# Splitting the memory rows of a cross-attention in four steps beside the units of the attention before it

## The chip, the core and the metric

The kernel runs on one core of a Trainium2 chip. Time is device time in microseconds (us) for one execution of the whole layer. The core has a matmul engine (TensorE, PE in the profile, with its weight loads shown apart as PEld), a vector engine (VectorE, DVE), an activation engine (ScalarE, ACT), GpSimd (POOL) and a queue that issues transfers (SyncE, SP). Each engine takes its instructions in the order in which the program lists them for that engine; between engines they wait on semaphores.

## The reference, cut to what matters

One decoder layer on 512 tokens of width 1024, all in float32:

```
x = x + 0.5 * swiglu(rmsnorm(x), gate, up, down)               # FFN 1, hidden width 2816
h = rmsnorm(x); z = h @ w_in                                   # 2560 columns
y_a = spatial gating of z[:, :1024], groups of 64, chunks of 128
y_b = causal attention, 8 heads of 64, three dilations summed by their softmax denominators
x = x + concat(rmsnorm(y_a), rmsnorm(y_b)) @ w_out
h = rmsnorm(x); m = rmsnorm(mem) * mem_norm                    # mem: 256 rows of width 1024
x = x + softmax((h @ wq) @ (m @ wk).T / 16) @ (m @ wv) @ wo    # cross-attention, 4 heads
x = x + 0.5 * swiglu(rmsnorm(x), gate, up, down)               # FFN 2
out = rmsnorm(x)
```

The change concerns m: the 256 normalised rows of the memory, which the cross-attention needs for its keys and values and which depend on nothing that the layer computes before.

## The kernel before

Activations are held transposed: feature blocks of 128 on the partitions, tokens along the free axis. Every product is made three times: each operand is split into a high part (rounded to the matmul's format) and a low part (the rest), and `mm3` (L124 to L129) adds high by high, high by low and low by high in PSUM. A split costs one ACTIVATE on ACT for the high part (L103) and one subtraction on DVE for the low part (L104). Weights come in by `load_weight` (L109): a transfer on SP into `wraw`, then a split into `whi` and `wlo`; each of the three has 3 buffers, so a weight's buffers hold up the loads behind it until its low part has been made and its matmuls are done.

The stages follow each other as in the reference: FFN 1, `mixers`, `cross`, FFN 2. In `mixers` the heads are worked off in 32 units (4 head pairs m, 2 heads r of a pair, 4 blocks i of 128 query rows). A unit u goes through three functions, and the loop at L617 to L626 runs them with a lag:

- `scores(u)`: three matmuls of 256 to 512 columns into a PSUM bank `aux` (4 banks), then on DVE the mask and the row minimum (L523), on ACT the exponential (L527), on DVE the reciprocal (L530) and the scaling (L531).
- `transposes(u - 3)`: up to four PE transposes (L539) into another `aux` bank, and a split into `pt` on ACT and DVE.
- `values(u - 4)`, for every second unit: 6 or 12 matmuls of 256 columns into an `aux` bank, and a split into `yH` and `yL` (L570, L571) with a square (L574). After the last block of a head pair, at the units 7, 15, 23 and 31, the squares are added up; two of these additions run on POOL (L170).

L523 is thus what gives a score's PSUM bank back, and its block of 128 columns (i = 0) marks the start of four units in the trace: the first, fifth, ninth and so on.

Two pieces of work lie between the units. At `u == 12` `qk_transpose(1)` makes queries and keys of the second half of the heads (L453). At `u == 16` `mem_split` (L389) loads the memory rows in four transfers (L393, tile `mraw`, which takes the four buffers of tag `qk` when `qk_transpose` has read them for the last time), and for each of the four transfers multiplies two row blocks by the norm's gain and factor on DVE (L395, 2 instructions), and splits the pair into `mH` (ACT, L103) and `mL` (DVE, L104). It returns the lists that `cross` (L673) uses for its values and keys.

The order of the instructions on each engine is not written out by hand: a scheduler lays it out when the program is built, by what is ready in its own estimate of time, and the earlier line of the program goes first among what is ready. So the first half of the output projection (`mix_out`, part 0, L631 to L640: 8 weight loads, 96 matmuls of 512 columns in all, an addition to `x` on DVE for each of 8 blocks), which needs only the gating's output, is found in the trace between the attention's matmuls; so are its splits of weights (`wlo`) on DVE.

Of the kernel before, what the change touches and what calls it, by code (L numbers as in the profile page):

```python
# [17 lines left out]
F32 = mybir.dt.float32  # L18
# [6 lines left out]
P = 128  # L25
S = 512
D = 1024
KD = D // P
# [4 lines left out]
NM = 256  # L33
# [5 lines left out]
LAG = 3  # L39
WARM = 20  # L40
SB = 6
LINE = 512

FILL = 56
# [10 lines left out]
def body(tc, I, out):  # L55
    nc = tc.nc
    from contextlib import ExitStack
    ctx = ExitStack()
    with ctx:
# [27 lines left out]
        def gcol(off, k):  # L87
            return gains[:, off + k:off + k + 1]
# [13 lines left out]
        def split(hi, lo, src):  # L102
            ins = nc.scalar.activation(hi, src, AF.Copy)  # L103
            nc.vector.tensor_sub(lo, src, f32(hi))  # L104
            return ins
# [281 lines left out]
            return h[0][k][:, ts], h[1][k][:, ts]  # L387

        def mem_split(pool, big, mR):  # L389
            mH, mL = (big.tile([P, KD, NM], F32R, name=n, tag="t8", bufs=4) for n in ("mH", "mL"))  # L390
            for k in range(0, KD, 2):
                raw = pool.tile([P, 2, NM], F32, name="mraw", tag="qk", bufs=4)
                nc.sync.dma_start(raw, I["memT"][k:k + 2].rearrange("k p n -> p k n"))  # L393
                for j in range(2):
                    nc.vector.scalar_tensor_tensor(raw[:, j], raw[:, j], gcol(G_MEM, k + j), mR,  # L395
                                                   op0=ALU.mult, op1=ALU.mult)
                split(mH[:, k:k + 2], mL[:, k:k + 2], raw)
            return [mH[:, k] for k in range(KD)], [mL[:, k] for k in range(KD)]

        def mixers(norm, cs, big):  # L400
            col = []
            hshape = [P, 8, 64]
            with tc.tile_pool(name="mix", bufs=1) as mp:
                lng = mp.tile([P, S], F32, name="lng", tag="s2", bufs=SB)
                lnb = mp.tile([P, S], F32, name="lnb", tag="s2", bufs=SB)
                nc.sync.dma_start(lng, I["ln"][0:1, :].to_broadcast([P, S]))
# [23 lines left out]
                qk = {}  # L430
# [18 lines left out]
                def qk_transpose(b):  # L449
                    for m in range(4):  # L450
                        ps = aux_tile()
                        for t in range(NT):
                            nc.tensor.transpose(ps[:, t * P:(t + 1) * P],  # L453
                                                qk[t][:, m * P:(m + 1) * P], ident_b)
                        if m >= 2:
                            hi, lo = h_tile("qkH"), h_tile("qkL")
                            split(hi, lo, ps)
                            kT[2 * b + m % 2] = (hi, lo)
                            continue


                        qT[2 * b + m % 2] = []
                        for r in range(2):
                            hi, lo = h_tile("qkH"), h_tile("qkL")
                            rows, other = (slice(x * 64, (x + 1) * 64) for x in (r, 1 - r))
                            for x in (hi, lo):
                                nc.gpsimd.memset(f32(x[other]), 0.0)
                            split(hi[rows], lo[rows], ps[rows])
                            qT[2 * b + m % 2].append((hi, lo))
# [19 lines left out]
                for t in range(NT):  # L489
# [3 lines left out]
                    nc.vector.tensor_sub(vt, vt, mu[:, t, :, None].to_broadcast(hshape))  # L493
                    sq = mp.tile([P, S], F32, name="vsq", tag="s2", bufs=SB)
                    nc.scalar.activation(sq, V[:, t], AF.Square)
# [18 lines left out]
                def scores(u):  # L514
                    m, r, i = units[u]
                    n = (i + 1) * P
                    N = max(n, 256)
                    sc = aux_tile()
                    mm3(sc[:, :N], qT[m][r], kT[m], (slice(None), slice(i * P, (i + 1) * P)),
                        (slice(None), slice(0, N)), True, True)  # L520
                    s = mp.tile([P, S], F32, name="s", tag="s2", bufs=SB)
                    nmx = sm.tile([P, 1], F32, name="nmx", tag="nmx")
                    nc.vector.tensor_tensor_reduce(  # L523
                        out=s[:, :n], in0=sc[:, :n], in1=const[:, C_MASK + S - n:C_MASK + S],
                        scale=-ATT_SCALE, scalar=3e38, op0=ALU.add, op1=ALU.min, accum_out=nmx)
                    Z = sm.tile([P, 1], F32, name="Z", tag="Z")
                    nc.scalar.activation(s[:, :n], s[:, :n], AF.Exp, bias=nmx, scale=-1.0,  # L527
                                         accum_out=Z)
                    rz = sm.tile([P, 1], F32, name="rz", tag="rz")
                    nc.vector.reciprocal(rz, Z)  # L530
                    nc.vector.tensor_scalar_mul(s[:, :n], s[:, :n], rz)  # L531
                    prob[u] = s

                def transposes(u):
                    m, r, i = units[u]
                    s = prob.pop(u)
                    tr = aux_tile()
                    for kt in range(i + 1):
                        nc.tensor.transpose(tr[:, kt * P:(kt + 1) * P],  # L539
                                            s[:, kt * P:(kt + 1) * P], ident)  # L540
                    if i % 2 == 0:
                        pts[m, r, i // 2] = tuple(
                            mp.tile([P, 4, 256], F32R, name="pt", tag="t4", bufs=4)
                            for _ in range(2))
                        for p in pts[m, r, i // 2]:
                            nc.gpsimd.memset(f32(p[:, i + 1, 0:P]), 0.0)
                    pt = pts[m, r, i // 2]
                    c0 = (i % 2) * P
                    split(pt[0][:, :i + 1, c0:c0 + P], pt[1][:, :i + 1, c0:c0 + P],
                               tr.rearrange("p (k c) -> p k c", k=4)[:, :i + 1])  # L550

                def values(u):
                    m, r, i = units[u]
                    if i % 2 == 0:
                        return
                    rows = slice(r * 64, (r + 1) * 64)
                    pv = aux_tile()
                    pt = pts.pop((m, r, i // 2))
                    for kt in range(i + 1):
                        mm3(pv[:, :256], (vH[kt], vL[kt]), pt,  # L560
                            (slice(None), slice(m * P, (m + 1) * P)),
                            (slice(None), kt), kt == 0, kt == i)
                    if r == 0 and i == 1:
                        yH[4 + m], yL[4 + m] = h_tile("yH"), h_tile("yL")
                        sqs[m] = base.tile([P, S], F32, name="sqb", tag="sq" if m else "sqacc",
                                           bufs=3 if m else 1)
                    o = pv[rows, :256]
                    c = slice((i - 1) * P, (i + 1) * P)
                    g = gcol(G_OB, m)[rows]
                    nc.scalar.activation(yH[4 + m][rows, c], o, AF.Copy, scale=g)  # L570
                    nc.vector.scalar_tensor_tensor(yL[4 + m][rows, c], o, g,  # L571
                                                   f32(yH[4 + m][rows, c]),
                                                   op0=ALU.mult, op1=ALU.subtract)
                    nc.scalar.activation(sqs[m][rows, c], o, AF.Square)  # L574
                    if r == 1 and i == NT - 1:
                        stats.take(sqs[m])

                def gate_mix():
# [11 lines left out]
                    for t in range(NT):  # L590
                        sq = mp.tile([P, S], F32, name="usq", tag="s2", bufs=SB)
                        nc.scalar.activation(sq, U[:, t], AF.Square, accum_out=ssa[:, t:t + 1])
# [24 lines left out]
                for u in range(LAG, nu + LAG + 1):  # L617
                    if u == nu // 2 - LAG - 1:
                        qk_transpose(1)
                    if u == nu // 2:  # L620
                        mem["split"] = mem_split(mp, big, mem["R"])
                    if u < nu:
                        scores(u)
                    transposes(u - LAG) if u - LAG < nu else None
                    if u > LAG:
                        values(u - LAG - 1)  # L626
# [20 lines left out]
        mem = {}  # L647
# [157 lines left out]
        with tc.tile_pool(name="big", bufs=1) as big:  # L805
            y = mixers(n2, cs[0], big)
            cross(n3, y, mem["split"], n4, big)
# [86 lines left out]
```

## Time and profile before

| | |
|---|---|
| median of 3 runs | 1131.15 us (1131.06 to 1132.29) |
| the profiled execution: its own time | 1132.03 us |
| its span, first to last instruction | 1130.3 us |
| mean granted clock of PE | 0.994 |
| PE busy | 1113.1 us, 98% of the span |
| DVE busy | 592.8 us, 52% |
| ACT busy | 424.6 us, 38% |
| POOL busy | 74.8 us, 7% |
| transfers | 110.79 MB, 98 GB/s on average |

Times in the trace count from the first instruction. The profiled execution is one execution with a time of its own, which lies 0.88 us above the median of the runs; 1.73 us of it lie outside the span. Busy shares are averages over all stages. The attention of `mixers` lies between about 490 and 563 us. In a list of instructions, a row holds the start, the duration, the engine, the line, the operation, what is written and read, and the shape; a bracket behind it gives the idle time of the engine before it and what ended it. In a table of stretches, a row holds the stretch, its length, the busy time of PE, PEld, DVE, ACT and POOL with the instructions in brackets, the granted clock, the share of the transfer engines and GB/s.

### The profile page before, as it was taken

What the parts mean: (1) busy time and instruction counts of PE and PEld (TensorE: products, weight loads), DVE (VectorE), ACT (ScalarE), POOL (GpSimd) and SP (SyncE); (2) the same over time, 40 slices, a digit from 0 to 9 for tenths busy, and PEclk for the clock granted to TensorE, in tenths of its full rate; (3) what the DMA queues carried; (4) which work ended last, traced back from release to release, by engine and by line L of the source; (5) the groups of instructions that cost most, each with busy time, mean ns of one, the idle gap of its engine ahead of it and who ended that gap; (6) DMA issues with size and microseconds to landing.
All of it is one profiled execution on the core that took longest, in us unless ns stands there. A gap on an engine that the chain in (4) does not pass through costs nothing. (4 is left out here: it accounts for less than half of the span.)

```text
span 1130.3 us, 13961 instructions
## 1 busy us (share of the span) xinstructions
PE 1113.1 (98%) x5472; PEld 934.5 (83%) x5472; DVE 592.8 (52%) x1027; ACT 424.6 (38%) x672; POOL 74.8 (7%) x98
## 2 busy tenths in 40 slices
PE   9999999999999999999999999999999999999996
PEld 7788888888888888887878988778888888888996
DVE  4544533444444447579897555455444334455542
ACT  6332312232234333567655344333232222333420
POOL 2000100000002200011121000120000000000011
PEclk9999999999999999999999999999999999999998
DMA  6322333222233422111136421232332333223511
GB/s 220 112 94 89 114 91 131 99 93 93 77 92 111 149 93 95 38 48 38 57 103 205 150 71 60 60 109 80 107 93 66 102 113 109 96 93 114 155 64 38
DMA packets 39698, 110.79 MB, mean 98 GB/s; under 512 B 4432, under 2 KB 9296, under 8 KB 39632
## 3 DMA queue, kind: packets, MB, share of 16 engines
q1 hardware_dynamic: 39632, 109.89, 30.5%
q8 instruction: 43, 0.70, 0.2%
q14 instruction: 23, 0.19, 0.1%
HBM read 107.78 MB, written 2.10 MB: 97 GB/s over the span
## 5 line engine op out<-in xcount | busy, mean ns | idle before, releaser
L103 ACT ACTIVATE whi<-wraw 128x1024 fp32r<-128x1024 f32 (+2 forms) x213 | 202.8, 953 | 519.6 <-PE acc L128 292.5
L104 DVE TENSOR_TENSOR wlo<-wraw,whi 128x1024 fp32r<-128x1024 f32 (+2 forms) x213 | 236.9, 1114 | 162.7 <-ACT whi L103 162.5
L127 PE MATMUL acc<-hH,whi 128*128 128x512 f32 x768 | 300.6, 391 | 0.0
L128 PE MATMUL acc<-hL,whi 128*128 128x512 f32 x768 | 299.2, 390 | 0.8 <-DVE hL L203 0.7
L129 PE MATMUL acc<-hH,wlo 128*128 128x512 f32 x768 | 299.1, 389 | 0.5 <-DVE wlo L104 0.5
L128 PEld LDWEIGHTS acc<-hL,whi 128*128 128x128 f32 x768 | 144.2, 188 | 32.2 <-DVE hL L203 2.2
L127 PEld LDWEIGHTS acc<-hH,whi 128*128 128x128 f32 x768 | 144.2, 188 | 30.9 <-issue 0.5
L129 PEld LDWEIGHTS acc<-hH,wlo 128*128 128x128 f32 x768 | 144.2, 188 | 30.6 <-DVE wlo L104 1.0
L127 PE MATMUL acc<-hidH,whi 128*128 128x512 f32 (+1 forms) x308 | 115.5, 375 | 0.0
L129 PE MATMUL acc<-hidH,wlo 128*128 128x512 f32 (+1 forms) x308 | 115.2, 374 | 0.0
L128 PE MATMUL acc<-hidL,whi 128*128 128x512 f32 (+1 forms) x308 | 115.2, 374 | 0.0
L170 POOL TENSOR_TENSOR sq<-sq 128x512 f32<-128x512 f32 (+1 forms) x39 | 49.4, 1266 | 774.2 <-ACT sq L178 773.7
L247 DVE TENSOR_TENSOR u<-acc,R 128x512 f32<-128x512 f32 x44 | 30.4, 690 | 121.6 <-PE acc L129 121.6
L243 DVE TENSOR_TENSOR gp<-acc,R 128x512 f32<-128x512 f32 x44 | 30.4, 691 | 85.5 <-PE acc L129 81.7
L127 PEld LDWEIGHTS acc<-hidH,whi 128*128 128x128 f32 x308 | 58.0, 188 | 10.3
L129 PEld LDWEIGHTS acc<-hidH,wlo 128*128 128x128 f32 x308 | 58.0, 188 | 10.3
L128 PEld LDWEIGHTS acc<-hidL,whi 128*128 128x128 f32 x308 | 58.0, 188 | 10.3
L127 PE MATMUL acc<-whi,hH 128*128 128x512 f32 x160 | 62.5, 390 | 0.0
L129 PE MATMUL acc<-whi,hL 128*128 128x512 f32 x160 | 62.3, 389 | 0.0
L128 PE MATMUL acc<-wlo,hH 128*128 128x512 f32 x160 | 62.3, 389 | 0.0
L230 DVE SCALAR_TENSOR_TENSOR x<-acc,x 128x512 f32<-128x512 f32 (+1 forms) x40 | 23.3, 584 | 73.9 <-PE acc L129 73.9
L178 ACT ACTIVATE sq<-x 128x512 f32<-128x512 f32 (+1 forms) x48 | 26.1, 551 | 40.7 <-DVE x L230 38.0
(213 smaller groups left out, 1490.0 us busy)
## 6 DMA issues: line engine op xcount, KB each, us to landing
wraw<-up SPq DMA_DIRECT2D x44, 512.0 KB, 3.5
wraw<-gate SPq DMA_DIRECT2D x43, 512.0 KB, 3.4
wraw<-down SPq DMA_DIRECT2D x28, 384.0 KB, 3.1
wraw<-w_in SPq DMA_DIRECT2D x20, 512.0 KB, 3.5
wraw<-down SPq DMA_DIRECT2D x28, 320.0 KB, 2.8
wraw<-w_out SPq DMA_DIRECT2D x16, 256.0 KB, 2.6
wraw<-wv SPq DMA_DIRECT2D x8, 512.0 KB, 3.5
wraw<-wk SPq DMA_DIRECT2D x8, 512.0 KB, 4.5
```

The lines of the kernel that those rows point to most:

```text
L103: ins = nc.scalar.activation(hi, src, AF.Copy)
L104: nc.vector.tensor_sub(lo, src, f32(hi))
L127: nc.tensor.matmul(ps, lhsT=aH, rhs=bH, start=start, stop=False)
L128: nc.tensor.matmul(ps, lhsT=aH, rhs=bL, start=False, stop=False)
L129: nc.tensor.matmul(ps, lhsT=aL, rhs=bH, start=False, stop=stop)
L170: nc.gpsimd.tensor_add(self.parts[0], self.parts[0], sq)
L178: nc.scalar.activation(sq, src, AF.Square)
L230: nc.vector.scalar_tensor_tensor(X[d][:, tok], acc, 0.5, X[d][:, tok], op0=ALU.mult, op1=ALU.add)
L243: nc.vector.tensor_mul(gp, ps[0], R)
L247: nc.vector.tensor_mul(u, ps[1], R)
```

## The change

`mem_split` becomes a generator. Its first call allocates `mH` and `mL`, issues all four transfers one behind the other and enters the lists of `mH` and `mL` in `mem`; each of the four calls that follow does one of the four pairs of row blocks: two L395 multiplications, the ACT copy and the DVE subtraction. The first call stands at unit 16, where the whole function stood; the others stand at the units 20, 23, 26 and 29, in the loop ahead of that unit's `scores`. No instruction is added or taken away.

```diff
--- before.py
+++ after.py
@@ -39,6 +39,8 @@
 LAG = 3
 WARM = 20
 SB = 6
+
+MEM_AT = (16, 20, 23, 26, 29)
 LINE = 512
 
 FILL = 56
@@ -387,15 +389,19 @@
             return h[0][k][:, ts], h[1][k][:, ts]
 
         def mem_split(pool, big, mR):
+
             mH, mL = (big.tile([P, KD, NM], F32R, name=n, tag="t8", bufs=4) for n in ("mH", "mL"))
+            raws = []
             for k in range(0, KD, 2):
-                raw = pool.tile([P, 2, NM], F32, name="mraw", tag="qk", bufs=4)
-                nc.sync.dma_start(raw, I["memT"][k:k + 2].rearrange("k p n -> p k n"))
+                raws.append(pool.tile([P, 2, NM], F32, name="mraw", tag="qk", bufs=4))
+                nc.sync.dma_start(raws[-1], I["memT"][k:k + 2].rearrange("k p n -> p k n"))
+            mem["split"] = [mH[:, k] for k in range(KD)], [mL[:, k] for k in range(KD)]
+            for k, raw in zip(range(0, KD, 2), raws):
+                yield
                 for j in range(2):
                     nc.vector.scalar_tensor_tensor(raw[:, j], raw[:, j], gcol(G_MEM, k + j), mR,
                                                    op0=ALU.mult, op1=ALU.mult)
                 split(mH[:, k:k + 2], mL[:, k:k + 2], raw)
-            return [mH[:, k] for k in range(KD)], [mL[:, k] for k in range(KD)]
 
         def mixers(norm, cs, big):
             col = []
@@ -618,7 +624,9 @@
                     if u == nu // 2 - LAG - 1:
                         qk_transpose(1)
                     if u == nu // 2:
-                        mem["split"] = mem_split(mp, big, mem["R"])
+                        steps = mem_split(mp, big, mem["R"])
+                    if u in MEM_AT:
+                        next(steps, None)
                     if u < nu:
                         scores(u)
                     transposes(u - LAG) if u - LAG < nu else None
```

## The prediction

> **What bounds the kernel now.** I read the page first: shares, slices, granted clock.
>
> ```profile
> span 1130.3 us, 13961 instructions
> PE 1113.1 (98%) x5472; PEld 934.5 (83%) x5472; DVE 592.8 (52%) x1027; ACT 424.6 (38%) x672; POOL 74.8 (7%) x98
> ...
> PE   9999999999999999999999999999999999999996
> ...
> DVE  4544533444444447579897555455444334455542
> ```
>
> PE carries the whole span, so a change is worth what it does to PE's idle time and to PE's clock. DVE is at half load on average, but in the slices 17 to 20, the attention, it is as full as PE. Next the list of waits of PE: of all its idle time one wait is of size in this stage.
>
> ```profile
> PE aux L127 <- DVE nmx L523: 2.1, 1, 2.1
> ```
>
> The timelines of PE and of DVE around that wait show where it lies (idle time before the instruction in brackets).
>
> ```profile
> 521.08 0.40 PE L128 MATMUL acc<-yL,whi 128*128 128x512 f32 x1
> ...
> 523.26 0.40 PE L128 MATMUL acc<-yL,whi 128*128 128x512 f32 x1
> 525.74 0.39 PE L127 MATMUL aux<-pt,vH 128*128 128x256 f32 x1 [2.08 <-DVE nmx L523]
> ```
>
> ```profile
> 518.41 0.67 DVE L523 CUSTOM_DVE_ANT_0 s<-aux,const 128x512 f32<-128x512 f32 x1
> ...
> 521.98 1.27 DVE L395 SCALAR_TENSOR_TENSOR mraw<-mraw,gains,R 128x256 f32<-128x256 f32 x3
> 523.39 0.69 DVE L104 TENSOR_TENSOR mL<-mraw,mH 128x512 fp32r<-128x512 f32 x1
> 524.00 0.48 DVE L395 SCALAR_TENSOR_TENSOR mraw<-mraw,gains,R 128x256 f32<-128x256 f32 x1
> 524.40 0.68 DVE L104 TENSOR_TENSOR mL<-mraw,mH 128x512 fp32r<-128x512 f32 x1
> 525.00 0.48 DVE L395 SCALAR_TENSOR_TENSOR mraw<-mraw,gains,R 128x256 f32<-128x256 f32 x1
> 525.39 0.28 DVE L523 CUSTOM_DVE_ANT_0 s<-aux,const 128x128 f32<-128x128 f32 x1
> ...
> 533.86 0.29 DVE L523 CUSTOM_DVE_ANT_0 s<-aux,const 128x128 f32<-128x128 f32 x1
> ...
> 540.16 0.29 DVE L523 CUSTOM_DVE_ANT_0 s<-aux,const 128x128 f32<-128x128 f32 x1 [0.15 <-PE aux L129]
> ...
> 547.85 0.29 DVE L523 CUSTOM_DVE_ANT_0 s<-aux,const 128x128 f32<-128x128 f32 x1
> ```
>
> The L523 rows of 128 columns open the units 16, 20, 24 and 28. Between unit 15 (518.41) and unit 16 (525.39) DVE works off nearly the whole memory split in one burst. Unit 16's scores lie in their PSUM bank meanwhile, the values of older units find no bank, and PE stands for 2.08 us after the output projection's matmuls (`acc<-yL,whi`) that it still had. Tables of stretches give the rest: cut at the units first, then finely behind the gap (PE, PEld, DVE, ACT, POOL, then the clock).
>
> ```profile
> 514.30:525.40 11.10, 9.36 (x61) 7.92 (x59) 10.82 (x35) 8.32 (x22) 0.81 (x4) 1.00 0.17 51
> 525.40:533.90 8.50, 7.82 (x40) 6.31 (x41) 7.53 (x26) 5.92 (x16) 1.05 (x5) 0.80 0.00 1
> 533.90:540.20 6.30, 5.89 (x38) 4.66 (x39) 6.14 (x23) 4.90 (x14) 1.92 (x5) 1.00 0.00 0
> 540.20:547.90 7.70, 7.70 (x52) 6.52 (x51) 7.16 (x25) 6.33 (x18) 0.77 (x4) 1.00 0.23 71
> 547.90:563.20 15.30, 15.12 (x100) 13.04 (x99) 12.54 (x35) 9.82 (x26) 2.27 (x5) 1.00 0.18 59
> ```
>
> ```profile
> 523.70:525.70 2.00, 0.00 (x0) 0.00 (x0) 2.00 (x7) 0.74 (x3) 0.00 (x0) 1.00 0.00 0
> 525.70:526.90 1.20, 1.16 (x7) 1.01 (x8) 1.20 (x5) 1.20 (x5) 0.03 (x1) 0.99 0.00 0
> 526.90:530.30 3.40, 3.40 (x14) 2.67 (x13) 3.22 (x11) 1.60 (x5) 0.36 (x2) 0.50 0.01 2
> 530.30:533.90 3.60, 3.26 (x23) 2.62 (x23) 2.81 (x10) 2.93 (x8) 0.67 (x3) 1.00 0.00 0
> ```
>
> Behind the gap the clock is halved for 3.40 us: 1.70 us of PE work lost. From 530.30 to 540.20 PE idles 0.34 + 0.41 = 0.75 us more. **PE's ledger: 2.08 + 1.70 + 0.75 = 4.53 us**, the most that taking the burst away can give here. **DVE's ledger** is smaller. While PE stood, DVE was full; it idled 0.97 us from 525.40 to 533.90 (8.50 - 7.53), mostly waiting on the slow PE, 0.54 from 540.20 to 547.90, and 2.76 in the attention's end from 547.90 on, where PE is the full engine (15.12 of 15.30).
>
> **The change part by part.** *The burst goes.* Its instructions, by tile, with minimum, median and maximum in ns:
>
> ```profile
> L395 DVE SCALAR_TENSOR_TENSOR mraw<-mraw,gains,R x8: 467/476/480, 515.3 to 525.0; 128x256 f32<-128x256 f32 x8
> ...
> L103 ACT ACTIVATE mH<-mraw x4: 617/618/631, 520.7 to 525.5; 128x512 fp32r<-128x512 f32 x4
> L104 DVE TENSOR_TENSOR mL<-mraw,mH x4: 684/689/694, 521.4 to 526.3; 128x512 fp32r<-128x512 f32 x4
> ```
>
> Back to back, a row's cost is from its start to the next start: L395 0.40 (524.00 to 524.40), the subtraction 0.60 (524.40 to 525.00). A step is 2 x 0.40 + 0.60 = 1.40 us of DVE, all four 5.60. Seven L395 and three subtractions run between unit 15 and 16, give or take one: 7 x 0.40 + 3 x 0.60 = 4.60 us; without them unit 16 opens at about 525.39 - 4.60 = 520.8.
>
> *The steps come back.* Nothing is added, so I follow the lead over the trace of before. At unit 16 it is 4.60. Up to unit 20, the last subtraction (0.60) and the 0.97 us of idle DVE fall out too, and the first step goes in: 4.60 + 0.60 + 0.97 - 1.40 = 4.77. The steps at 23 and 26 take 1.40 each: 3.37 at unit 24, 1.97 at unit 28, or 2.51 if DVE's 0.54 idle there is filled. The last step falls where DVE idles 2.76 and PE is full. The eighth L395, at 515.3 and so ahead of unit 15, gives 0.40 more if unit 15 itself comes earlier by it. So the lead at the attention's end is 2.51 + 0.40 = **2.9** if the last step is hidden, and 1.97 - 1.40 + 0.40 = **0.97** if it isn't and nothing is filled. I take 2.9, the high end: between 540.2 and 563.2 PE is busy 22.82 of 23.00 us and DVE 19.70, so a step there delays DVE work which PE isn't yet waiting for, and a lead that reaches unit 24 is kept. Against PE's ledger it leaves 4.53 - 2.9 = 1.6 us of idling, about 0.4 per step, for the new gaps.
>
> *The cover of the steps* is the output projection's matmuls between the units; they need `wlo` from DVE.
>
> ```profile
> 504.13 0.68 DVE L104 TENSOR_TENSOR wlo<-wraw,whi 128x512 fp32r<-128x512 f32 x1
> ...
> 539.26 0.68 DVE L104 TENSOR_TENSOR wlo<-wraw,whi 128x512 fp32r<-128x512 f32 x1
> ```
>
> For 35 us DVE makes no `wlo`, so PE lived on products with `whi` and a few left over with `wlo`; those from 521.08 to 523.66 ran under the burst. Without the burst they are left for the first steps: at most 2.58 us of cover against 2 x 1.40. If that cover is gone, a step stands bare on PE, at most 1.40.
>
> *Waits on the pairs.* A subtraction waits for its ACT copy (0.62), with DVE's whole queue behind it. With other work laid between, as in the burst, it costs 0; bare, four times 0.62 = 2.5. I take 0: no row of the burst above has idle time before it. A copy waits for its two L395 (0.80), with exponentials and `pt` copies behind it; it is the same wait as before, 0.
>
> *Transfers and SP.* The four issues stay at unit 16 and in SP's order.
>
> ```profile
> SPq L393 <- PE aux L453: 6.5, 1, 6.5
> ```
>
> ```profile
> 511.44 1.92 SPq L393 DMA_DIRECT2D mraw<-memT  x4
> 540.00 7.74 SPq L116 DMA_DIRECT2D wraw<-w_out  x3
> ```
>
> They wait for `qk_transpose`'s last read, as they would after the change, and the first L395 reads from 515.3 on, long before unit 20; the next issue, a weight, waits for the `wlo` of 539.26 and not for them. Cost 0. `mH` is first read at 588.71 (`acc<-whi,mH`), the last step ends at about 550: 38 us of slack, 0.
>
> ```profile
> 588.71 0.39 PE L127 MATMUL acc<-whi,mH 128*128 128x512 f32 x1
> ```
>
> *A neighbour on POOL.* L395 and the subtraction read two operands from SBUF. Such an instruction beside a POOL addition is seen later in this trace:
>
> ```profile
> 577.03 1.38 POOL L170 TENSOR_TENSOR sq<-sq 128x512 f32<-128x512 f32 x1 [21.20 <-ACT sq L178]
> ```
>
> ```profile
> 577.18 1.78 DVE L644 TENSOR_TENSOR x<-x,yo 128x512 f32<-128x512 f32 x1
> ```
>
> ```profile
> 533.79 1.29 POOL L170 TENSOR_TENSOR sqb<-sqb 128x512 f32<-128x512 f32 x1 [1.53 <-ACT sqb L574]
> ...
> 549.83 1.29 POOL L170 TENSOR_TENSOR sqb<-sqb 128x512 f32<-128x512 f32 x1 [2.05 <-ACT sqb L574]
> ```
>
> L644 takes 1.78 beside it against its usual 0.69, so 1.09 more. The burst met none of the two `sqb` additions; they stand at unit 20 and unit 29, where two of the steps go. Bounds 0 and 2 x 1.09 = 2.2; I take 0.3, nearer to 0, since a step must start inside 1.3 us and the second one has idle DVE around it. The Trainium skill, SBUF — State Buffer, "Who interferes with whom", says that a DVE instruction with two SBUF inputs contends with a GpSimd instruction that reads SBUF, and that whichever starts first holds the port. The 1.78 agrees, and by this rule a step that starts within an addition pays its remainder, at most 1.29; the sum would be 1.0 lower for one full hit.
>
> **Sum**: 2.9 - 0.3 = 2.6 us off the profiled execution's own 1132.03 (span 1130.3, 1.73 around it): 1129.4. That execution is 0.88 above the median. If the offset is of all profiled executions, the median falls to 1131.15 - 2.6 = 1128.55; if it is the halved clock, which the median runs then lacked, the time is 1129.4. I forecast **1128.8**, 0.21% under the median; own range 1127.9 to 1129.7.
>
> **The rivals.** *A wash:* DVE sets the pace from unit 12 to the end, its 5.60 us are only shifted, and the gain is what the slow clock cost it, 0.97, or less: 1130.2 to 1131.2. For it: 10.82 of 11.10 busy; against it: DVE's idle time from 540 on.
>
> *All of PE's ledger:* the fillers cover every step and the scheduler also moves a `wlo` ahead: 4.53, so 1131.15 - 4.53 = 1126.6. Against it: it needs DVE over 95% busy to the end.
>
> *Slower, two gaps for one:* at the steps 23 and 26 the `whi` products are used up and `wlo` is starved, now by steps instead of a burst. PE then stands twice, and each gap that comes near 2.08 us halves the clock as the one before did, 2.08 + 1.70 = 3.78 each. One gap more than before gives 1131.15 + 3.78 = 1134.9. It decides as soon as a step's 1.40 and a DVE neighbour (a `wlo`, 0.60) meet uncovered, 2.0 us. Against it: the products left over by the burst. On the clock the Trainium skill, TensorE: Matmul & The Clock Gate, "Part 1: The HAM clock gate", says that the clock halves after about 3.4 us of idle; by that rule no gap of 2 us costs more than itself, and PE's ledger would be 2.83. This trace differs (2.08 us sufficed), and it decides.
>
> *Not as said:* the scheduler lays steps elsewhere, or the new order costs later what it gives here: about 1131.
>
> **How the numbers follow.** Forecast 0.55, wash 0.20, all of the ledger 0.12, slower 0.09, not as said 0.04. 0.2% is 2.26 us and about what a measurement tells from no change; faster means under 1128.9. Two thirds of the forecast (0.37) and the full ledger: faster 0.49. The last third, the wash and the fourth rival: same 0.42. Slower 0.09. The range takes in the ledger and the wash, with a little for unknown waits: 1126.4 to 1131.6; the slower case is left out.
>
> **What would show it.** Right: no `mraw` instruction on DVE between the L523 of units 15 and 16, which lie about 2.4 us apart; the 2.08 gap gone and the clock at 1.00 throughout; unit 24 about 3.4 to 3.8 us early, unit 28 between 2 and 3, PE full from there. The wash shows an L523 of unit 28 within 1 us of before, and gaps of above 1 us at the steps. Wrong: a stretch of halved clock anywhere from 520 to 560, an L395 or `mL` above 1 us beside L170, or PE idle behind 563.

## The result, and the profile after

| | median | runs |
|---|---|---|
| before, beside the changed kernel | 1131.49 us (1130.5 to 1132.9) | 22 |
| changed | 1133.08 us (1132.3 to 1133.71) | 22 |
| ratio changed to before | 1.0014, 95% interval 1.0007 to 1.002 | |

The changed kernel is 1.6 us slower, where 1128.8 was forecast and the range ended at 1131.6. The interval of the ratio lies above 1 throughout, so the direction is clear of the noise. The profiled execution has 1133.24 us, 1131.5 of it the span; its granted clock is 0.995 (before 0.994). The ratios here and below are of runs in the chip's fast state; the one slow run among all of them is a run of e1 that took 1300.16 us.

In the new file the lines of the attention lie lower: `mm3` is L129 to L131 (was L127 to L129), the split L105 and L106 (L103, L104), the weights' transfers L118 (L116), the POOL addition L172 (L170), the memory's transfers L397 (L393), the multiplication L402 (L395), `scores` L529 (L523), the transposes L545 (L539), the square behind the values L580 (L574).

The page, with shares and slices:

```profile
span 1131.5 us, 13958 instructions
...
PE 1112.1 (98%) x5472; PEld 934.2 (83%) x5472; DVE 593.2 (52%) x1027; ACT 424.6 (38%) x672; POOL 74.5 (7%) x98
...
DVE  4544533444444447589887455455444334445542
```

The busy times are those of before, within 1 us, and each engine has as many instructions as before. So the time lies in where PE idles, and the first thing to look at is whether the gap ahead of unit 16 is gone. It is. These are the waits of PE from 520 to 570 us (in total, times, longest); before, one wait of 2.1 us for `nmx` stood at their head.

```profile
PE aux L129 <- ACT sqb L580: 1.8, 2, 1.1
PE aux L545 <- DVE nmx L529: 1.6, 3, 0.6
```

And this is DVE's timeline, to be held against that of before:

```profile
518.44 0.67 DVE L529 CUSTOM_DVE_ANT_0 s<-aux,const 128x512 f32<-128x512 f32 x1
...
519.64 0.47 DVE L402 SCALAR_TENSOR_TENSOR mraw<-mraw,gains,R 128x256 f32<-128x256 f32 x1
520.14 0.47 DVE L402 SCALAR_TENSOR_TENSOR mraw<-mraw,gains,R 128x256 f32<-128x256 f32 x1
...
521.32 0.27 DVE L529 CUSTOM_DVE_ANT_0 s<-aux,const 128x128 f32<-128x128 f32 x1
...
528.42 0.29 DVE L529 CUSTOM_DVE_ANT_0 s<-aux,const 128x128 f32<-128x128 f32 x1 [0.15 <-PE aux L131]
...
531.21 0.76 DVE L402 SCALAR_TENSOR_TENSOR mraw<-mraw,gains,R 128x256 f32<-128x256 f32 x1
...
536.62 0.27 DVE L529 CUSTOM_DVE_ANT_0 s<-aux,const 128x128 f32<-128x128 f32 x1
...
544.48 0.29 DVE L529 CUSTOM_DVE_ANT_0 s<-aux,const 128x128 f32<-128x128 f32 x1
545.04 1.75 DVE L106 TENSOR_TENSOR mL<-mraw,mH 128x512 fp32r<-128x512 f32 x1
```

The units 16, 20, 24 and 28 open at 521.32, 528.42, 536.62 and 544.48. That is 4.07, 5.44, 3.54 and 3.37 us earlier than before, close to the walk of the prediction (4.60, 4.77, 3.37, 2.51). The attention ends early too. Its last matmul with values, after and before:

```profile
556.46 0.28 PE L131 MATMUL aux<-pt,vL 128*128 128x256 f32 x1
```

```profile
562.35 0.28 PE L129 MATMUL aux<-pt,vL 128*128 128x256 f32 x1
```

It starts 5.9 us earlier, and yet the kernel ends later. The table of stretches of the changed kernel, cut at its own units (PE, PEld, DVE, ACT, POOL, the clock, the transfers' share, GB/s), shows at what price:

```profile
514.30:521.30 7.00, 7.00 (x50) 6.34 (x49) 6.87 (x26) 5.72 (x17) 0.81 (x4) 1.00 0.26 82
521.30:528.40 7.10, 6.96 (x47) 5.94 (x45) 6.75 (x24) 6.65 (x19) 0.78 (x4) 1.00 0.00 1
528.40:536.60 8.20, 6.30 (x45) 5.35 (x43) 8.07 (x27) 6.26 (x19) 1.96 (x5) 1.00 0.00 0
536.60:544.50 7.90, 6.81 (x42) 5.36 (x42) 7.67 (x27) 6.63 (x19) 0.87 (x4) 1.00 0.01 2
544.50:551.00 6.50, 5.14 (x32) 3.93 (x33) 6.50 (x21) 4.69 (x13) 1.58 (x3) 1.00 0.01 1
551.00:556.50 5.50, 4.78 (x35) 4.04 (x34) 5.17 (x11) 3.11 (x9) 0.39 (x2) 1.00 0.16 48
556.50:569.00 12.50, 12.50 (x61) 10.01 (x61) 7.38 (x25) 3.97 (x7) 0.00 (x0) 1.00 0.36 106
```

From 528.40 on PE idles 1.90, 1.09, 1.36 and 0.72 us of a stretch, 5.07 in all, at full clock; DVE is nearly full there (27.41 of 28.10), so the attention has little room to go quicker, and PE has nothing else to do. Before, PE was full from unit 24 on (7.70 of 7.70, 15.12 of 15.30). What it did then can be read from the rows of the instructions that read or write `yH`, on PE the output projection's matmuls (same columns without POOL; its products with `yL` aren't in these rows). Before:

```profile
530.00:540.00 10.00, 0.50 (x1) 0.19 (x1) 0.96 (x2) 1.12 (x3) 0.99 0.00 0
540.00:550.00 10.00, 3.28 (x9) 1.60 (x9) 1.45 (x3) 1.21 (x3) 1.00 0.24 81
550.00:560.00 10.00, 3.98 (x12) 2.13 (x12) 1.44 (x3) 1.41 (x3) 1.00 0.11 36
560.00:570.00 10.00, 6.07 (x19) 3.32 (x18) 0.49 (x1) 0.47 (x1) 1.00 0.20 69
```

After:

```profile
530.00:540.00 10.00, 0.00 (x0) 0.00 (x0) 1.39 (x3) 1.41 (x3) 1.00 0.00 0
540.00:550.00 10.00, 0.46 (x1) 0.19 (x1) 0.99 (x3) 0.94 (x2) 1.00 0.01 2
550.00:560.00 10.00, 2.75 (x9) 1.47 (x9) 1.46 (x3) 1.40 (x3) 1.00 0.24 79
560.00:570.00 10.00, 8.64 (x28) 4.92 (x27) 0.00 (x0) 0.00 (x0) 1.00 0.29 80
```

Between 530 and 550 PE had 10 matmuls of this kind before, and 1 after (15 and 2 with the products of `yL`). They are not lost; they are done later, alone, behind the attention. And the reason is DVE's order. The low parts of the weights in the changed kernel, in DVE's timeline of `wlo`:

```profile
504.16 0.68 DVE L106 TENSOR_TENSOR wlo<-wraw,whi 128x512 fp32r<-128x512 f32 x1
...
553.39 0.67 DVE L106 TENSOR_TENSOR wlo<-wraw,whi 128x512 fp32r<-128x512 f32 x1
```

For 49 us DVE makes no `wlo`; before it was 35 (504.13 to 539.26). Its inputs don't hold it up: ACT starts the high parts of the next three weights at 506.69, 514.07 and 522.22, 0.63 us each, so the first `wlo` of these could be made long before 553.39 (in e9, below, the same one is made at 519.57). The queue of the transfers stands behind it. Its longest wait, after and before (from 505 to 560 us):

```profile
SPq L118 <- DVE wlo L106: 42.5, 3, 40.7
```

```profile
SPq L116 <- DVE wlo L104: 43.2, 5, 26.6
```

So of the 96 matmuls of the projection's first half, 85 had begun before when the attention's last matmul started, and 57 after (counted in PE's timeline). The 28 that are missing come behind it. The 96th starts at 565.61 before and at 567.91 after.

One more count closes the account. For each matmul I took the distance to the next one's start, less an allowance in proportion to its columns (0.229 us for 512, which is what matmuls of 512 columns need in a row), and added this up; a halved clock is contained in it. The sums hang on the allowance: with the median distance of each shape in its place, they are 24.69 and 25.89 us. The differences between the kernels change by 0.35 at most.

| PE time lost (us) | 0 to 490 | 490 to 520 | 520 to 530 | 530 to 540 | 540 to 550 | 550 to 566 | 566 to 640 | 640 to the end | all |
|---|---|---|---|---|---|---|---|---|---|
| before | 5.30 | 4.60 | 4.77 | 3.13 | 1.75 | 2.12 | 3.80 | 9.16 | 34.62 |
| after | 5.35 | 4.57 | 2.61 | 3.44 | 4.11 | 3.42 | 3.20 | 9.13 | 35.83 |

The difference, 1.21 us, is that of the two spans; the medians differ by 1.59, since the profiled execution of before lies 0.54 above its median and the one after 0.16. Between 520 and 530 the change gave 2.16 us back: the 3.78 of the gap and the slow clock, less a new gap of 1.05 at 529.3 and smaller ones. From 530 to 566 it cost 3.97 in gaps of up to 1.1 us, and 0.60 came back behind.

### The profile page after: what moved, and what is told of

Same layout as the page of the kernel before. It is cut to its first block, busy times and chain, and to the rows that moved or that the text cites. A ratio compares the mean times of both kernels' runs of the same rounds, so it can differ in the third digit from the quotient of the medians.

```text
span 1131.5 us, 13958 instructions
## 1 busy us (share of the span) xinstructions
PE 1112.1 (98%) x5472; PEld 934.2 (83%) x5472; DVE 593.2 (52%) x1027; ACT 424.6 (38%) x672; POOL 74.5 (7%) x98
## 5 line engine op out<-in xcount | busy, mean ns | idle before, releaser
L105 ACT ACTIVATE whi<-wraw 128x1024 fp32r<-128x1024 f32 (+2 forms) x213 | 202.7, 953 | 520.8 <-PE acc L130 294.0
L106 DVE TENSOR_TENSOR wlo<-wraw,whi 128x1024 fp32r<-128x1024 f32 (+2 forms) x213 | 236.9, 1114 | 162.2 <-ACT whi L105 161.7
L129 PE MATMUL acc<-hH,whi 128*128 128x512 f32 x768 | 300.6, 391 | 0.1
L131 PE MATMUL acc<-hH,wlo 128*128 128x512 f32 x768 | 299.1, 389 | 0.5 <-DVE wlo L106 0.5
L129 PEld LDWEIGHTS acc<-hH,whi 128*128 128x128 f32 x768 | 144.2, 188 | 30.9 <-ACT hH L204 0.5
L131 PEld LDWEIGHTS acc<-hH,wlo 128*128 128x128 f32 x768 | 144.2, 188 | 30.8 <-DVE wlo L106 1.0
L129 PE MATMUL acc<-hidH,whi 128*128 128x512 f32 (+1 forms) x308 | 115.5, 375 | 0.0
L131 PE MATMUL acc<-hidH,wlo 128*128 128x512 f32 (+1 forms) x308 | 115.2, 374 | 0.0
L172 POOL TENSOR_TENSOR sq<-sq 128x512 f32<-128x512 f32 (+1 forms) x39 | 49.4, 1266 | 779.7 <-ACT sq L180 779.2
L131 PEld LDWEIGHTS acc<-hidH,wlo 128*128 128x128 f32 x308 | 58.0, 188 | 10.3
L129 PEld LDWEIGHTS acc<-hidH,whi 128*128 128x128 f32 x308 | 58.0, 188 | 10.2
L129 PE MATMUL acc<-whi,hH 128*128 128x512 f32 x160 | 62.5, 390 | 0.0
L131 PE MATMUL acc<-whi,hL 128*128 128x512 f32 x160 | 62.3, 389 | 0.0
```

What stands on the lines that cost most here:

```text
L129: nc.tensor.matmul(ps, lhsT=aH, rhs=bH, start=start, stop=False)
L131: nc.tensor.matmul(ps, lhsT=aL, rhs=bH, start=False, stop=stop)
L172: nc.gpsimd.tensor_add(self.parts[0], self.parts[0], sq)
```

## The experiments

My theory after this reading, called "starved filler" in the expectations and S here: the steps starve the filler, which is the projection's matmuls that PE puts between the attention's. What an experiment is measured "against" is the kernel before, run beside it; behind the ratio stands its 95% interval. The steps carry the program rank of the attention's loop, the projection's weights that of `mix_out`, which stands behind it. The scheduler puts a step into any place of DVE's queue that opens between two units, and these were the places of `wlo`. The rivals: the steps' places in the loop (a stage that is only badly chosen), the port that DVE and POOL share, and the rewriting of the function itself.

The order that the scheduler wrote for DVE shows the rank at work (numbers are the scores of units, W a `wlo`, m a multiplication of memory rows, L an `mL`):

```
before    9 W 10 .. 13 m 14 15 m m L m m m L m L m 16 17 L 18 .. 23 W 24 25 W 26 27 W 28 .. 31 W W W
changed   9 W 10 .. 13 m 14 15 m m 16 17 L m 18 19 L 20 21 m 22 23 m m 24 25 L 26 27 m 28 L 29 30 31 W W W
```

Spread out, the steps sit in every opening up to unit 28. As a burst they were over at unit 17 and left the openings at 23, 25 and 27 to `wlo`.

### e1: the new function, all four steps at unit 16

```diff
+                    if u == nu // 2:
+                        for _ in steps:
+                            pass
```

> Starved filler (the steps rank ahead of the projection's low parts, so PE's filler matmuls are left for the end): all four steps stand at unit 16 again, only the loads still go first; the low parts get the places they had before, and the time is that of the kernel before, within 0.5 us, with some 86 of the projection's first 96 matmuls done at the attention's last value. If the loads or the earlier allocation cost the time, it stays with the changed kernel, 1.2 to 1.6 us above the kernel before.

Measured: 1131.74 us against 1131.88, ratio 0.9999 (0.999 to 1.0008). The wait and, in the table of stretches, the clock are back, each in one line:

```profile
PE aux L129 <- DVE nmx L529: 2.1, 1, 2.1
```

```profile
527.20:530.60 3.40, 3.40 (x14) 2.68 (x13) 3.12 (x11) 1.54 (x5) 0.33 (x2) 0.53 0.01 2
```

The rewritten function costs nothing that can be measured. What the change does, it does by spreading the steps.

### e2: the steps in the output projection, behind the blocks 1, 3, 5 and 7

The four transfers stay at unit 16, but into buffers of `h`, since those of tag `qk` are given up with the attention. They issue earlier by that, from 504.7 us on and not from 511.5, and so they do in e9 and e10. A step is then called in `mix_out`, so it has the rank of the weights.

```diff
-MEM_AT = (16, 20, 23, 26, 29)
+MEM_AT = (16,)
...
-                raws.append(pool.tile([P, 2, NM], F32, name="mraw", tag="qk", bufs=4))
+                raws.append(hp.tile([P, S], F32, name="mraw", tag="h").rearrange("p (k n) -> p k n", k=2))
...
                     if part == 0:
                         nc.vector.tensor_add(X[d], acc, X[d])
+                        if d % 2:
+                            next(mem["steps"], None)
```

> The loads stay at unit 16 (into other buffers); the four steps are put behind the projection's blocks 1, 3, 5 and 7, so that they rank below the low parts. Starved filler: the 2.08 us gap and the halved clock stay away, the low parts come near units 23 to 27 as before, and the time falls 1 to 3 us below the kernel before. Bare steps (each step costs PE a gap wherever it stands) or the port beside POOL: the same DVE work in the same stage, so as slow as the changed kernel, 1.2 to 1.6 us above the kernel before.

Measured: 1129.1 us against 1131.88, ratio 0.9975 (0.9964 to 0.9985). The attention's last matmul starts at 558.26, 1.8 later than in the changed kernel, but 88 of the 96 matmuls have begun by then, and the 96th starts at 560.89. With the same steps and the same work, their rank moved and the loads earlier, the time falls by 4 us from the changed kernel, to 2.8 below the kernel before. S had said 1 to 3 below, the rivals as slow as the changed kernel. That the loads are not the reason, e10 will show.

### e3: the changed kernel, with the weights of the first half in the loop

Now the other way round: the steps stay, and the weights' rank is raised. The eight loads of part 0, splits and all, are called at the units 4, 7, 10 and so on to 25.

```diff
+                    if (u - 4) % 3 == 0 and len(early) < KD:
+                        early.append(load_weight(I["w_out"][0, len(early)], [4, P]))
...
-                    w = load_weight(I["w_out"][part, d], [4, P])
+                    w = early[d] if part == 0 else load_weight(I["w_out"][part, d], [4, P])
```

> The changed kernel with its four steps where they are; only the loads and splits of the projection's eight weights are named earlier in the program, beside the units 4, 7, 10 to 25, so that they rank ahead of the units that follow. Starved filler: low parts come at units 13, 19 and 23, more than 70 of the 96 matmuls are done at the last value, and the time falls at least 1 us below the changed kernel, to the kernel before or under it. Bare steps or port: within 0.5 us of the changed kernel.

Measured: 1130.95 us against 1131.88, ratio 0.9991 (0.9982 to 1.0). That is 2.1 under the changed kernel's 1133.08; 85 matmuls have begun at the attention's last (561.22), as many as before. Two edits on different code, one that lowers the steps and one that lifts the weights, take the loss away. Against the kernel before, e3 gains too little to be told from nothing: its attention ends only 1.1 us earlier.

### e4: the changed kernel without additions on POOL

```diff
-                stats = Stats(4, tail=1)
+                stats = Stats(4, tail=4)
```

The squares are then summed by eight more one-column matmuls on PE, and no POOL addition lies beside DVE.

> The changed kernel without the two additions of squares on POOL; the four squares are summed by 8 more one-column matmuls (0.11 us each, 0.9 us, at the attention's end). Port: the subtraction of 1.75 us falls to 0.68 and the multiplication of 0.76 to 0.47, 1.4 us less, so 0.5 us or more below the changed kernel. Starved filler: the attention ends earlier by that, the filler doesn't, and the time stays or rises, 0 to 0.9 us above the changed kernel.

Measured: 1134.48 us against 1131.88, ratio 1.0024 (1.0014 to 1.0034). The 1.75 us subtraction is gone; the groups by tile (minimum, median and maximum in ns), of the changed kernel and of this one:

```profile
L106 DVE TENSOR_TENSOR mL<-mraw,mH x4: 673/680/1747, 522.4 to 545.0; 128x512 fp32r<-128x512 f32 x4
```

```profile
L106 DVE TENSOR_TENSOR mL<-mraw,mH x4: 672/678/682, 522.5 to 545.1; 128x512 fp32r<-128x512 f32 x4
```

Yet the time is 1.4 above the changed kernel's, more than the 0.9 that S had left room for. The price of the matmuls was taken too low. Behind the attention, in the changed kernel and in this one:

```profile
556.58 0.95 PE L188 MATMUL aux<-ones,sqb 128*128 128x1 f32 x8
```

```profile
556.08 1.84 PE L188 MATMUL aux<-ones,sqb 128*128 128x1 f32 x16
```

Each of the eight has two records in the trace, so there are 32 where there were 16; from start to next start they take 3.33 us of PE against 1.54, 1.8 more and not 0.9. Less that, what the missing collisions gave back is about 0.4 us (an estimate, 1.8 - 1.4). The number of matmuls begun at the attention's end is the same, 57. So the collision is real, 1.07 us of DVE, and it isn't what made the kernel 1.6 us slower.

### e5: e2 and e3 together

> Steps in the output projection (as in the run before that put them there) and the projection's weights named early too. Starved filler: low parts come at the units 7, 11, 13, 15 and 21, the projection's first half is done soonest of all, and the time is that of the steps in the projection alone, 1129.1 us, or up to 1.5 us less. If the gain there came only from moving the steps past the attention's units, nothing is added: 1129.1 within 0.5 us.

Measured: 1129.34 us against 1131.6, ratio 0.998 (0.9971 to 0.9989), no better than e2 alone (0.9975). Both readings had allowed that, so the run doesn't choose between them. The filler is all used up by 556.87, before the attention's last matmul at 562.24, and PE waits later for a weight of the second half:

```profile
PE acc L131 <- DVE wlo L106: 2.3, 1, 2.3
```

### e6: the kernel before, with e3's weights in the loop

> The kernel before, its split in one burst at unit 16, with the projection's weights named early. Starved filler: the low parts come at the units 17 to 21 and not at 23 to 27, but the burst still stands ahead of unit 16 with the 2 us gap behind it, so it gains at most 1 us on the kernel before. If naming the weights early is worth something by itself whatever the split does, it gains as much as it gave the changed kernel, 2.1 us.

Measured: 1134.91 us against 1131.6, ratio 1.0032 (1.002 to 1.0045). S had expected a gain of at most 1 us and its rival one of 2.1; it lost 3.3, and both were wrong. The 96 matmuls are all under way at 556.97, 8.6 us sooner than before, and the projection's second half begins during the attention. Then, in the table of stretches behind the attention:

```profile
572.00:580.00 8.00, 8.00 (x37) 6.60 (x36) 7.18 (x10) 5.49 (x10) 2.76 (x2) 1.00 0.20 66
580.00:588.00 8.00, 1.88 (x7) 0.82 (x6) 8.00 (x10) 4.48 (x7) 3.17 (x4) 0.81 0.00 0
588.00:592.00 4.00, 4.00 (x10) 3.17 (x11) 3.26 (x3) 0.02 (x1) 1.57 (x1) 0.54 0.59 167
```

```profile
PE acc L129 <- DVE wlo L104: 4.7, 1, 4.7
```

PE runs dry from 580 to 588, with DVE full, and the clock halves with it. The filler that the attention ate is missing where DVE has the projection's second half, the additions to `x` and the next norm to do. So more filler ahead wasn't better without end: the matmuls are a stock, and both stages live on it. This reading came after the run, and no further run tests it.

### e7: the changed kernel with the last four steps at the units 28, 29, 30, 31

```diff
-MEM_AT = (16, 20, 23, 26, 29)
+MEM_AT = (16, 28, 29, 30, 31)
```

> The changed kernel with its steps beside the units 28, 29, 30 and 31 in place of 20, 23, 26 and 29. Starved filler by rank: the scheduler runs a step as soon as it finds a place, ahead of any low part, whatever unit it is named at; the order on DVE hardly changes and the time is that of the changed kernel, 1133.1 within 0.5 us. If the units at which the steps are named set where they run (my forecast's walk), the steps leave the middle of the attention and the time falls 1 us or more.

Measured: 1132.9 us against 1131.6, ratio 1.0012 (1.0003 to 1.0021), the changed kernel again (1.0014). The groups by tile show why, in the first and last start of the multiplications:

```profile
L402 DVE SCALAR_TENSOR_TENSOR mraw<-mraw,gains,R x8: 462/467/771, 515.2 to 542.2; 128x256 f32<-128x256 f32 x8
```

A step that is called at unit 28 begins at 515.2, ahead of unit 15, as it does when called at unit 20 (515.37). The four unit numbers of the change hardly matter: a step goes out when its row has landed and DVE has an opening. They only give a rank: a step goes behind the scores that are named before it if those are ready, and ahead of every `wlo`.

### e8: the price of the work itself

The kernel before, with the memory rows copied to `mH` on ACT without gain and norm, and `mL` set to zero on POOL. The 5.60 us of DVE are gone; this leaves out the memory's norm and the low half of its split, and it shows a floor, not a kernel.

```diff
-                for j in range(2):
-                    nc.vector.scalar_tensor_tensor(raw[:, j], raw[:, j], gcol(G_MEM, k + j), mR,
-                                                   op0=ALU.mult, op1=ALU.mult)
-                split(mH[:, k:k + 2], mL[:, k:k + 2], raw)
+                nc.scalar.activation(mH[:, k:k + 2], raw, AF.Copy)
+                nc.gpsimd.memset(f32(mL[:, k:k + 2]), 0.0)
```

> The kernel before without the split's work on DVE: the memory rows are copied to the high part as they are, without gain and norm, and the low part is set to zero on POOL, so the output isn't the layer's; PE and ACT do as much as before. It prices the 5.60 us of DVE in this stage. Starved filler: the low parts come from unit 15 on, no gap and no halved clock, 3 to 4.5 us below the kernel before. If the DVE work of the split costs only the burst's gap and clock, 2.08 to 3.78 us.

Measured: 1127.69 us against 1131.6, ratio 0.9967 (0.9955 to 0.998). Without any DVE work for the memory 3.9 us are to be had.

### e9 and e10: the steps behind the last four blocks, and behind the first four

Both are e2 with another condition, `if d > 3` in e9 and `if d < 4` in e10. In e10 the first step ranks ahead of the weights of all blocks from 1 on, the last ahead of those from 4 on; in e9 all four rank behind the first five of the eight weights.

> The steps behind the output projection's blocks 4, 5, 6 and 7. Starved filler by rank: the low parts of blocks 0 to 4 rank ahead of every step; they come at the units 15 and 25, the gap of 2 us stays away, and the time is that of the steps behind the blocks 1, 3, 5 and 7 or up to 1 us to either side: 1128.1 to 1130.1. If only leaving the attention's units counted, the same as the next run.

> The steps behind the output projection's blocks 0, 1, 2 and 3: out of the attention's units as in the run before it, but ahead of the low parts of blocks 4 to 7 and of those of blocks 1 to 3 that come after. Starved filler by rank: no low part comes between unit 9 and unit 31, as in the changed kernel, fewer than 65 of the 96 matmuls are done at the last value, and the time is the changed kernel's, 1133.1 within 0.7 us. If leaving the units is what helped, 1129.1 within 0.7 us.

Measured, both against 1131.7: e9 1127.91 us, ratio 0.9969 (0.9956 to 0.9982), 0.2 below the range that I had given; e10 1133.2 us, ratio 1.0013 (1.0004 to 1.0022). e10's time was the expected one; its count, 70 matmuls at the attention's end, lies above the 65 that I had set as the limit. The `wlo` rows of DVE's timeline in e9:

```profile
519.57 0.67 DVE L106 TENSOR_TENSOR wlo<-wraw,whi 128x512 fp32r<-128x512 f32 x1
...
538.31 0.67 DVE L106 TENSOR_TENSOR wlo<-wraw,whi 128x512 fp32r<-128x512 f32 x1
...
551.07 0.67 DVE L106 TENSOR_TENSOR wlo<-wraw,whi 128x512 fp32r<-128x512 f32 x1
```

And the matmuls of the projection in e9, by the same rows as above:

```profile
530.00:540.00 10.00, 2.36 (x6) 1.14 (x6) 0.94 (x2) 1.40 (x3) 1.00 0.00 0
540.00:550.00 10.00, 2.69 (x8) 1.25 (x7) 1.45 (x3) 0.93 (x2) 1.00 0.09 29
550.00:560.00 10.00, 3.82 (x12) 2.09 (x13) 0.96 (x2) 0.94 (x2) 1.00 0.21 52
```

The longest time without a `wlo` is 18.7 us, the filler trickles through the whole attention, 14 matmuls between 530 and 550, and 94 of the 96 have begun at its last matmul (559.83). By the count of lost PE time it has 30.21 us against 34.62 before. With one condition of e2 changed, and the same buffers and early loads in both, e10 gives the changed kernel's loss again and e9 comes to within 0.2 us of e8, which leaves the work out: where the steps rank against the weights settles the time.

All twelve kernels side by side, by the start of the projection's 96th matmul:

| | attention's last matmul | begun of 96 by then | 96th matmul | time |
|---|---|---|---|---|
| e8, no DVE work | 558.74 | 93 | 559.33 | 1127.69 |
| e9, behind blocks 4 to 7 | 559.83 | 94 | 560.18 | 1127.91 |
| e2, behind blocks 1, 3, 5, 7 | 558.26 | 88 | 560.89 | 1129.1 |
| e3, weights lifted | 561.22 | 85 | 564.31 | 1130.95 |
| before | 562.35 | 85 | 565.61 | 1131.49 |
| e1, all at 16 | 562.65 | 85 | 565.90 | 1131.74 |
| e10, behind blocks 0 to 3 | 560.49 | 70 | 567.28 | 1133.2 |
| e7, units 28 to 31 | 555.93 | 57 | 567.37 | 1132.9 |
| changed | 556.46 | 57 | 567.91 | 1133.08 |
| e4, no POOL sums | 555.96 | 57 | 568.75 | 1134.48 |
| e5, e2 and e3 | 562.24 | 96 | 556.87 | 1129.34 |
| e6, before with weights lifted | 563.97 | 96 | 556.97 | 1134.91 |

In the first ten rows time follows the 96th matmul within the noise (e10, e7 and the changed kernel can't be told apart), and not the attention's end: the kernels whose attention ends first are among the slowest. The last two have run out of filler and pay in the stage behind.

## Why the prediction was wrong

**What bounds, and PE's ledger: right.** The 2.08 us gap and the 3.40 us of halved clock came from the burst; e1 brings both back, and the clock of the changed kernel is at 1.00 in all stretches from 514 to 569. The ledger of 4.53 us as the most to be had is near what e8 (3.9) and e9 (3.8) got.

**DVE's walk: near up to unit 28, short at the attention's end.** The units opened 4.07, 5.44, 3.54 and 3.37 us early, where the walk had 4.60, 4.77, 3.37 and 2.51. It assumed the steps at their named units, which they don't keep (e7). By unit 28 DVE had done 5.0 us of steps, where the walk had 4.2, and it had made three `wlo` and one addition to `x` fewer than before (2.4 us); that two misses nearly offset each other is luck. The attention ended 5.9 us early, not 2.9, and that surplus was no gain. From 510 us to the end of its attention DVE made 6 `wlo` and 5 additions to `x` before, and 3 and 2 after. At 0.60 us from start to next start these six instructions are 3.6 us of the filler's work, put off.

**"A lead that reaches unit 24 is kept": the step that failed.** I made the lead of the attention at its end a gain in time. But the end of this stage is the later of two things, the attention and the 96 matmuls beside it, and the lead was bought from the second. What the steps do to the low parts of the weights is a term that the sum put at nothing. I argued from PE's 22.82 busy us of 23.00 between 540.2 and 563.2 that DVE's steps would lie under PE's work there. About 8 us of that work, 35 matmuls at 0.229 us, was the projection's, and it was there because DVE made a `wlo` at 539.26, which the burst, by being over early, had allowed. By spreading the steps the change took away the cover that I had counted on to hide them. The 5.9 us turned into 28 more matmuls left over: 39 of them stood behind the attention and took 11.45 us (556.46 to 567.91), where before 11 took 3.26. That is 8.2 us more, against 5.9.

**The cover of the steps: seen and mispriced.** I quoted the 35 us without a `wlo` and asked only whether leftover products would cover the first two steps, at most 1.40 each. The right question was what each step does to the next `wlo`: by the rule that the earlier program line goes first among what is ready, any step that is ready beats any `wlo`, so the first `wlo` had to come behind the last step. With the steps spread to unit 28 it had to fall behind unit 28. It did, at 553.39. The direction of this, if not its size, could have been read from the diff and the scheduler's rule.

**Waits and transfers at 0: half right.** No subtraction of a pair shows a wait for its copy in the changed kernel, and the `memT` transfers cost nothing (L397 issues at the same place, with the same 1.92 us). The next issue on SP did wait for a `wlo`, as I said, but I took its time, 540.00, for fixed; it became 554.12.

```profile
511.47 1.92 SPq L397 DMA_DIRECT2D mraw<-memT  x4
554.12 2.91 SPq L118 DMA_DIRECT2D wraw<-w_out  x3
```

**POOL as a neighbour: larger than taken, and not the cause.** Two steps met an addition of POOL, at 545.04 (1.75 against 0.68) and at 531.21 (0.76 against 0.47), 1.36 us in all where 0.3 was taken and 2.2 the bound.

```profile
530.40 1.29 POOL L172 TENSOR_TENSOR sqb<-sqb 128x512 f32<-128x512 f32 x1 [2.05 <-ACT sqb L580]
...
544.94 1.29 POOL L172 TENSOR_TENSOR sqb<-sqb 128x512 f32<-128x512 f32 x1 [1.75 <-ACT sqb L580]
```

That agrees with what was cited from the Trainium skill, SBUF — State Buffer, "Who interferes with whom": the subtraction began 0.10 us into the addition and paid 1.07 of the 1.19 that were left of it. But e4 took the collisions away, and by its trace they are worth about 0.4 us of time.

**The rivals.** The slower one had the right victim, `wlo` starved by steps, and the wrong price and place: two gaps of 2 us with a halved clock, 3.78 each. The clock didn't halve in this stage; the loss came in small gaps, none above 1.1 us. It was given a chance of 0.09, on the argument of the burst's leftover products, which last to unit 20 and hardly further (9 projection matmuls from 520 to 530, then 2 up to 550). "Not as said" had half of the truth too, in that the scheduler lays the steps elsewhere. The wash was right that DVE sets the attention's pace, but unit 28 didn't stay within 1 us of before, as it said; like the forecast, it left out that a full DVE has the filler to feed as well. And the range left the slower case out, although no row of before bounded what the filler would lose.

**The signs.** "No `mraw` on DVE between units 15 and 16" was wrong as a sign: two multiplications still lie there (519.64, 520.14). The gap, the clock and unit 24 came as said, unit 28 was further ahead (3.37 against 2 to 3), and with all of them the kernel was slower. Of the signs of being wrong one appeared, the `mL` of 1.75 us beside POOL's addition, and it wasn't the reason. What I had put down as signs were signs of the attention; the only one that bore on the end was "PE full from there", and that one failed.

## What to carry to other kernels

Where two engines are full in one stage and a second piece of work fills the bound engine's gaps, a lead in the first piece is no time: ask which instructions of the other full engine feed the filler, and what the change puts ahead of them. Under a scheduler that goes by program order, where work is called is its rank, not its place. In this kernel the spread work belonged below most of what feeds the filler (e9: 1127.91 us, 3.8 under the kernel before), and lifting the feeder instead, with the burst left as it was, drained the next stage's stock (e6: 3.3 us lost).

## What the hardware showed that I had not expected

A single gap of 2.08 us in a PE that was otherwise busy halved the clock for 3.4 us, in the kernel before and again in e1 (0.53, in a stretch that reaches a little past the slow part). In e5 a gap of 2.30 us did the same: the clock is 0.50 from 582.1 to 585.5. The changed kernel has more idle time in the attention, but in pieces of at most 1.1 us, and keeps 1.00. So does e9, with a larger piece than these in the projection's second half:

```profile
579.37 0.50 PE L131 MATMUL acc<-yH,wlo 128*128 128x512 f32 x1 [1.68 <-DVE wlo L106]
```

```profile
579.70:583.10 3.40, 3.00 (x13) 2.17 (x12) 3.40 (x5) 1.39 (x3) 1.43 (x2) 1.00 0.46 154
```

The Trainium skill, TensorE: Matmul & The Clock Gate, "Part 1: The HAM clock gate", puts the limit at about 3.4 us of idle; here 2.08 was enough, 1.68 was not, and where between them the limit lies no run shows. So 5.07 us of idle time between 528 and 556.5 in small pieces cost just those 5.07, whereas 2.08 in one piece cost 3.78.
